# Scan stage of a hybrid SSD / Fourier layer: PSUM banks dealt out anew between the filling matrix products and the state products

## The chip, the cores and the metric

The kernel runs on one core of a Trainium2 chip. The metric is device time of one execution in microseconds (us). The kernel before takes 2252.82 us, the median of three runs (2246.53 to 2255.43). All readings below come from one further execution under the hardware profiler. Engines: PE is TensorE (matrix products), PEld its loading of weights, DVE is VectorE, ACT is ScalarE, POOL is GpSimd, SP is the engine from whose queue the DMAs are issued.

## The reference, cut to what matters

One layer over 1024 latent tokens and 256 context tokens of width 1024. The input projection feeds a bidirectional chunked state-space scan, a Fourier branch and two gates:

```python
u = h @ w_in[i]                                   # x, B, C | dt | z | Fourier | gates
states   = einsum('bcsgn,bcsgj,bcsgjp->bcgjpn', bc, decay_to_end, xdt)   # per chunk of 128
entering = scan(carry * dec + st)                                        # chunk after chunk
y_diag   = einsum('bcgjls,bcsgjp->bclgjp', cb[:, :, :, None] * lmat, xdt)
y_off    = einsum('bclgn,bcgjpn,bclgj->bclgjp', cc, entering, exp(a_cum))
y = (y_diag + y_off + d_skip * x) * silu(z)       # then grouped RMSNorm
mix = (gate0 * (y @ w_ssd_out) + gate1 * (f_mix @ w_fft_out)) @ w_o
```

There are 8 groups of 4 heads with 64 channels each, 8 chunks of 128 latent tokens and 2 of context, and two directions. After it come the residual, a SwiGLU feed-forward layer and the last norm.

## The kernel before, in words

The kernel is written against a tile framework: a program order is given, pools with a fixed number of buffers hold the tiles, and a scheduler that simulates time sets the order of the instructions on every engine and the waits between engines. A wait is kept by PSUM bank, not by address: two accesses of different engines to one bank are put one behind the other. [...]

The scan stage (the code from `phB = ExitStack()` on) does three kinds of PE work together:

- Filling products. `fill_stream` yields one piece after another of the input projection that the scan itself does not wait for at once: 12 weight blocks of `tm_units` (z and Fourier columns, 256 wide, eight token tiles each, so 96 tiles), and then five gate blocks of `gate_units` (j = 10 to 14, two PSUM tiles of 512 columns each). A tile of 256 columns is 24 products (8 blocks of k, three split products L203, L204, L205 in `mm3`). The z tiles (`fill` to `zs`) are read by ACT (tanh, L802) and then by DVE (L803), 64 of them. The Fourier tiles (`fill` to `ust`) are read by ACT alone (L807), 32 of them. All these use `fill_ps`, a pool of three banks.
- State products (`state_b`): for every group and step i, two products (L881, L882) of 128x256 go to the two halves of one bank `st`, of which there is one. DVE reads it in eight instructions (L891), which carry the running state `S` on.
- Outputs. Per tick n (group g, chunk c): `y_load` issues the DMA of `abc`, a broadcast of 512 KB from L900 that has two buffers. `y_a` makes `cb` (L908) and `yo` (L910, L911) on PE. ACT works over `abc` in eight instructions (L915), DVE in one (L917), ACT takes the exponential (L918), and DVE multiplies it with `cb` into `G` (L920). `y_b` multiplies `G` by x into `yd` (L943), `y_b2` finishes the row on DVE, ACT and POOL, and `y_c` transposes it (`ytr`, L968). `cb`, `yo`, `yd` and `ytr` have one bank each.

Together these are 3 + 1 + 4 = 8 banks. The loop over the ticks calls `state_a`, `state_b`, `y_a`, `y_b`, `y_c` and, last in each tick, `run_fill`, which draws pieces of the filling stream. What comes earlier in program order has priority in the scheduler.

Of the kernel before, what the change touches and what calls it, by code (L numbers as in the profile page):

```python
# [9 lines left out]
F32 = mybir.dt.float32  # L10
# [5 lines left out]
P = 128  # L16
# [125 lines left out]
def _build(nc, tc, h, o, hook, stop, es):  # L142
# [6 lines left out]
    def pool(name, side="left", bufs=1, space=None):  # L149
        kw = {} if space is None else dict(space=space)  # L150
        return tc.tile_pool(name=name, bufs=bufs, side=side, reuse_waits="tile", **kw)
# [38 lines left out]
    def wload(src, cols=1024):  # L190
        raw = wp.tile([P, 1024], F32, name="wraw", bufs=NRAW)
        nc.sync.dma_start(out=raw[:, :cols], in_=src)
        return wsplit(raw, cols)
# [8 lines left out]
    def mm3(ps, a, b, start, stop):  # L202
        nc.tensor.matmul(ps, lhsT=a[0], rhs=b[0], start=start, stop=False)  # L203
        nc.tensor.matmul(ps, lhsT=a[0], rhs=b[1], start=False, stop=False)  # L204
        nc.tensor.matmul(ps, lhsT=a[1], rhs=b[0], start=False, stop=stop)  # L205

    def mm3m(dsts, a, start, stop):
        for i, j in ((0, 0), (0, 1), (1, 0)):
            for ps, b in dsts:
                nc.tensor.matmul(ps, lhsT=a[i], rhs=b[j], start=start and (i, j) == (0, 0),  # L210
                                 stop=stop and (i, j) == (1, 0))
# [564 lines left out]
    ppg_ = hstack.enter_context(pool("ppg", "left", space=PSUM))  # L776
    pb = phB.enter_context(pool("pb", "right"))
    ppb = phB.enter_context(pool("ppb", "right", space=PSUM))
# [4 lines left out]
    ZSB, FOFF = 12, 4  # L783

    def fill_ps():
        return ppg_.tile([P, 512], F32, name="fill", bufs=3)

    zs_of = {}

    def tm_units(wi):  # L790

        w = [wload(h["wzf"][wi, kh]) for kh in range(2)]
        for t in range(NT):
            ps = fill_ps()[:, :256]
            for k in range(KT):
                hi, lo = w[k // 4]
                wsl = slice((k % 4) * 256, (k % 4) * 256 + 256)
                tsl = slice(t * P, t * P + P)
                mm3(ps, (h_hi[k][:, tsl], h_lo[k][:, tsl]), (hi[:, wsl], lo[:, wsl]), k == 0, k == KT - 1)
            if wi < NG:  # L800
                z = pb.tile([P, 256], F32, name="zs", bufs=ZSB)
                nc.scalar.activation(out=z, in_=ps, func=AF.Tanh, scale=0.5)  # L802
                nc.vector.scalar_tensor_tensor(out=z, in0=z, scalar=1.0, in1=ps, op0=ALU.add, op1=ALU.mult)  # L803
                zs_of[(wi, t)] = z
            else:
                u = pb.tile([P, 256], F32, name="ust", bufs=2)
                nc.scalar.copy(out=u, in_=ps)  # L807
                nc.sync.dma_start(out=s_u[wi - NG][:, t, :], in_=u)
            yield

    def gate_units(j):
        hi, lo = wload(h["wgate"][j])
        pss = [fill_ps() for _ in range(2)]
        for k in range(KT):
            sl = slice(k * P, k * P + P)
            mm3m([(pss[0], (h_hi[k][:, 0:512], h_lo[k][:, 0:512])), (pss[1], (h_hi[k][:, 512:], h_lo[k][:, 512:]))],
                 (hi[:, sl], lo[:, sl]), k == 0, k == KT - 1)
            if k == KT - 1:
                for hf in range(2):
                    gt = gtp.tile([P, 512], F32, name="gt", bufs=2)  # L820
                    nc.scalar.activation(out=gt, in_=pss[hf], func=AF.Tanh, scale=0.5)
                    nc.sync.dma_start(out=s_gate[j][:, 512 * hf:512 * hf + 512], in_=gt)
            if k % 2 == 1:
                yield
# [8 lines left out]
    class Group:  # L833
# [43 lines left out]
        def state_b(self, i):  # L877
            g, cf, cb = self.g, orf[i], orb[i]
            xf, xb = self.st.pop(i)
            st = ppb.tile([P, 512], F32, name="st", bufs=1)  # L880
            nc.tensor.matmul(st[:, 0:256], lhsT=self.Bt(cf), rhs=xf, start=True, stop=True)  # L881
            nc.tensor.matmul(st[:, 256:512], lhsT=self.Bt(cb), rhs=xb, start=True, stop=True)  # L882
            for d, S in ((0, self.Sf), (1, self.Sb)):
                sn = pb.tile([P, 256], F32, name=f"S{d}", bufs=9)
                sv_ = st[:, 256 * d:256 * d + 256]
                if i == 0:
                    nc.scalar.copy(out=sn, in_=sv_)
                else:
                    for j in range(HPG):
                        hd_ = slice(j * HD, j * HD + HD)  # L890
                        nc.vector.scalar_tensor_tensor(out=sn[:, hd_], in0=S[-1][:, hd_], scalar=decp[:, i, d, 4 * g + j:4 * g + j + 1],  # L891
                                                       in1=sv_[:, hd_], op0=ALU.mult, op1=ALU.add)
                S.append(sn)
# [85 lines left out]
    def fill_stream():  # L979
        yield from tm_units(0)  # L980
        jg = 2 * NGP
        for g in range(NG - 1):
            for _ in range(GSCHED[g]):
                yield from gate_units(jg)
                jg += 1
            if g in (1, 3, 5, 6):
                yield from tm_units(NG + (1, 3, 5, 6).index(g))
            yield from tm_units(g + 1)
        while jg < 15:
            yield from gate_units(jg)  # L990
            jg += 1

    fill = fill_stream()
# [228 lines left out]
    with pool("pd", "left") as pd_, pool("ppd", "left", space=PSUM) as ppd:  # L1222
# [29 lines left out]
        for kh in range(2):  # L1252
# [3 lines left out]
            for jd in range(8):  # L1256
                hi, lo = wload(h["wssd"][jd, kh])
                pss = [ppd.tile([P, 512], F32, name="dm", bufs=6) for _ in range(2)]
# [50 lines left out]
    with pool("pe", "left") as pe, pool("ppe", "left", space=PSUM) as ppe:  # L1309
# [3 lines left out]
        for dh in range(2):  # L1313
# [20 lines left out]
            for t in range(NT):  # L1334
                hf, tt = t // 4, t % 4
                ts_ = slice(tt * P, tt * P + P)
                ps = ppe.tile([P, 512], F32, name="em", bufs=3)
# [126 lines left out]
    for i in range(4):  # L1464
        t1, _, _, b22 = qd(i)
# [235 lines left out]
```

## Time and profile before

| | us |
|---|---|
| median of three runs | 2252.82 |
| the profiled execution | 2255.23 |
| its span on the core | 2253.5 |
| PE busy in the span | 2164.4 (96%) |
| PEld busy | 1809.4 (80%) |
| DVE busy | 1629.2 (72%) |
| ACT busy | 991.6 (44%) |
| POOL busy | 742.0 (33%) |

Times within the execution are counted from the start of the span. The scan stage lies between about 612 and 1165 us. An engine's row in a timeline gives the start, the length, the engine, the line, the operation and the tiles as out<-in; the bracket at its end is how long the engine sat idle before it, and what ended that.

### The profile page before, as it was taken

To read this page: it belongs to the slowest core of one execution; us is meant where nothing else is said; L and a number is where in the kernel's file an instruction comes from. 1 tells how busy PE (TensorE), PEld (TensorE's weight loads), DVE (VectorE), ACT (ScalarE), POOL (GpSimd) and SP (SyncE) were. 2 spreads that over 40 slices of the span, in tenths; PEclk is the share of its full clock that TensorE was granted. 3 is DMA by queue.
4 is the path that set the end of the run, shared out by engine and by line. 5 is a ranking of instruction groups with operands and counts; after the bars stand their busy time and mean duration, and the time that the engine had idled before them with its cause. 6 is when DMAs were issued, how large, how long until landed. Compare 5 with 4: busy or idle time off the path is not lost. (4 is left out here: it accounts for less than half of the span.)

```text
span 2253.5 us, 32731 instructions
## 1 busy us (share of the span) xinstructions
PE 2164.4 (96%) x11560; PEld 1809.4 (80%) x11560; DVE 1629.2 (72%) x2783; ACT 991.6 (44%) x2082; POOL 742.0 (33%) x610
## 2 busy tenths in 40 slices
PE   7999999999999999999999999998898999999997
PEld 1778888877889999999889887786676888887876
DVE  5888888997757777777636558826987567675578
ACT  4445444545345676676733212124422332334443
POOL 1532211010236455555521132144333333332222
PEclk8999999999999999999999999999899999999999
DMA  7222223333455455555454547541476234457765
GB/s 281 76 71 84 85 85 122 133 130 108 144 165 172 157 164 179 165 169 175 151 202 161 183 152 264 188 159 63 155 270 229 85 114 155 152 190 240 234 203 181
DMA packets 167101, 360.28 MB, mean 160 GB/s; under 512 B 17548, under 2 KB 57228, under 8 KB 166296
## 3 DMA queue, kind: packets, MB, share of 16 engines
q1 hardware_dynamic: 166936, 358.18, 47.7%
q8 instruction: 91, 1.49, 0.3%
q14 instruction: 74, 0.61, 0.1%
HBM read 267.34 MB, written 90.78 MB: 159 GB/s over the span
## 5 line engine op out<-in xcount | busy, mean ns | idle before, releaser
L199 POOL TENSOR_TENSOR wlo<-wraw,whi 128x1024 fp32r<-128x1024 f32 (+1 forms) x83 | 203.0, 2449 | 614.4 <-ACT whi L198 566.8
L203 PE MATMUL fill<-whi,hhi 128*128 128x256 f32 x768 | 222.4, 291 | 0.0
L198 ACT CAST whi<-wraw 128x1024 fp32r<-128x1024 f32 (+1 forms) x123 | 126.5, 1034 | 215.7 <-PE dm L210 82.9
L433 DVE SCALAR_TENSOR_TENSOR cv<-pad,vecs,cv 128x1282 f32<-128x1282 f32 (+1 forms) x128 | 211.0, 1678 | 9.1 <-ACT cv L430 8.7
L204 PE MATMUL fill<-wlo,hhi 128*128 128x256 f32 x768 | 215.8, 281 | 0.6 <-POOL wlo L199 0.6
L205 PE MATMUL fill<-whi,hlo 128*128 128x256 f32 x768 | 216.0, 282 | 0.0
L915 ACT ACTIVATE abc<-abc,a_all 128x128 f32<-128x128 f32 x512 | 157.8, 390 | 96.2 <-DMA abc<-s_a 93.4
L203 PE MATMUL fp<-m,oph 128*128 128x512 f32 x452 | 180.3, 400 | 12.5 <-ACT oph L1384 10.5
L205 PE MATMUL fp<-m,opl 128*128 128x512 f32 x452 | 180.4, 400 | 9.6 <-DVE opl L1385 6.7
L204 PE MATMUL fp<-m,oph 128*128 128x512 f32 x452 | 180.2, 399 | 0.0
L496 PE MATMUL mm<-tq,whi 128*128 128x512 f32 x480 | 153.9, 401 | 2.3 <-ACT whi L198 2.3
L203 PEld LDWEIGHTS fill<-whi,hhi 128*128 128x128 f32 x768 | 144.1, 188 | 2.2 <-ACT ust L807 0.4
L204 PEld LDWEIGHTS fill<-wlo,hhi 128*128 128x128 f32 x768 | 144.6, 188 | 1.6 <-POOL wlo L199 0.8
L205 PEld LDWEIGHTS fill<-whi,hlo 128*128 128x128 f32 x768 | 144.3, 188 | 0.5
L496 PE MATMUL mm<-hhi,whi 128*128 128x512 f32 x320 | 128.2, 402 | 3.4 <-DVE pad L572 3.4
L496 PE MATMUL mm<-hlo,whi 128*128 128x512 f32 x320 | 127.6, 399 | 0.0
L496 PE MATMUL mm<-hhi,wlo 128*128 128x512 f32 x320 | 127.6, 400 | 0.0
L203 PEld LDWEIGHTS fp<-m,oph 128*128 128x128 f32 x452 | 85.9, 190 | 34.2 <-ACT oph L1384 11.7
L205 PEld LDWEIGHTS fp<-m,opl 128*128 128x128 f32 x452 | 85.6, 189 | 33.8 <-DVE opl L1385 9.7
L917 DVE COPY_PREDICATED abc<-misc,abc 128x512 f32<-128x512 int32 x64 | 50.8, 793 | 85.0 <-ACT abc L915 84.8
L496 PEld LDWEIGHTS mm<-tq,whi 128*128 128x128 f32 x480 | 89.7, 189 | 23.7 <-ACT whi L198 3.4
L891 DVE SCALAR_TENSOR_TENSOR S<-S,ead,st 128x64 f32<-128x64 f32 x512 | 104.7, 271 | 0.0
(411 smaller groups left out, 5929.4 us busy)
## 6 DMA issues: line engine op xcount, KB each, us to landing
abc<-s_a SPq DMA_DIRECT2D x64, 512.0 KB
fraw<-in_wfi SPq DMA_DIRECT2D x44, 512.0 KB
wraw<-in_wxbc SPq DMA_DIRECT2D x32, 512.0 KB
dx<-in_wada SPq DMA_DIRECT2D x32, 512.0 KB
wraw<-in_wzf SPq DMA_DIRECT2D x24, 512.0 KB
gt<-s_gate SPq DMA_DIRECT2D x24, 512.0 KB
fi<-in_wfo SPq DMA_DIRECT2D x22, 512.0 KB
s_cw<-fo SPq DMA_DIRECT2D x44, 256.0 KB
```

Source lines behind the costliest of these rows:

```text
L198: nc.scalar.copy(out=hi[:, :cols], in_=raw[:, :cols])
L199: (eng or nc.gpsimd).tensor_tensor(out=lo[:, :cols], in0=raw[:, :cols], in1=hi[:, :cols].bitcast(F32), op=ALU.subtract)
L203: nc.tensor.matmul(ps, lhsT=a[0], rhs=b[0], start=start, stop=False)
L204: nc.tensor.matmul(ps, lhsT=a[0], rhs=b[1], start=False, stop=False)
L205: nc.tensor.matmul(ps, lhsT=a[1], rhs=b[0], start=False, stop=stop)
L433: nc.vector.scalar_tensor_tensor(out=v[:, :n], in0=pd[:, t:t + n], scalar=cwh[:, 5 * b + t:5 * b + t + 1], in1=v[:, :n], op0=ALU.mult, op1 ...
L496: nc.tensor.matmul(ps, lhsT=lhs[x], rhs=b[i][y], start=i == 0 and (x, y) == (0, 0), stop=i == 3 and (x, y) == (1, 0))
L891: nc.vector.scalar_tensor_tensor(out=sn[:, hd_], in0=S[-1][:, hd_], scalar=decp[:, i, d, 4 * g + j:4 * g + j + 1], in1=sv_[:, hd_], op0=AL ...
L915: nc.scalar.activation(out=abc[:, d, j, :], in_=abc[:, d, j, :], func=AF.Identity, scale=-1.0, bias=a_all[:, c, hd:hd + 1])
L917: nc.vector.copy_predicated(out=E, mask=tri_b.bitcast(mybir.dt.int32)[:, None, :].to_broadcast([P, HPG, P]), data=abc[:, 1])
```

## The change

Three edits, all in the scan stage. The filling pool shrinks from three banks to two, and two successive tiles of 256 columns of one weight block (t even, t odd) are now the two halves of one bank. The state products get a second bank. Gate blocks with odd j (11 and 13) take both banks of the state pool in place of the filling pool's. The count of banks stays eight (2 + 2 + 4), and no instruction is added or taken out; the scheduler makes a new order of them.

```diff
     def fill_ps():
-        return ppg_.tile([P, 512], F32, name="fill", bufs=3)
+        return ppg_.tile([P, 512], F32, name="fill", bufs=2)
+
+    def st_ps():
+        return ppb.tile([P, 512], F32, name="st", bufs=2)
...
         for t in range(NT):
-            ps = fill_ps()[:, :256]
+            if t % 2 == 0:
+                bank = fill_ps()
+            ps = bank[:, 256 * (t % 2):256 * (t % 2) + 256]
...
-        pss = [fill_ps() for _ in range(2)]
+        pss = [(st_ps if j % 2 else fill_ps)() for _ in range(2)]
...
-            st = ppb.tile([P, 512], F32, name="st", bufs=1)
+            st = st_ps()
```

Line numbers of the changed kernel are 3 higher than before from `tm_units` on and 5 higher from there to the end. Three places of the new order follow. The names are tiles with their numbers; `whi`, `wlo` are the split weights, `hhi`, `hlo` the split inputs.

PE at the start of the scan, before. Each `fill` number is one tile of 256 columns in a bank of its own:

```order
L203 MATMUL fill_4981<-whi_4971,hhi0_190 128x256 [waits DVE_49,Activation_49]
...
L203 MATMUL fill_5026<-whi_4971,hhi0_190 128x256 [waits DVE_49]
...
L203 MATMUL fill_5071<-whi_4971,hhi0_190 128x256
...
L203 MATMUL fill_5116<-whi_4971,hhi0_190 128x256 [waits DVE_49]
...
L908 MATMUL cb_5350<-cT_5322,bT_5320 128x128 [waits DMAHW5_49,DMAHW4_49]
L910 MATMUL yo_5352<-S0_4959,cT_5322 128x256
```

The first `cb` stands behind eight whole tiles. The same place now, where a `fill` number is a bank with two tiles:

```order
L203 MATMUL fill_5070<-whi_4971,hhi0_190 128x256 [waits DVE_49]
...
L203 MATMUL fill_4981<-whi_4971,hhi0_190 128x256 [waits DVE_49]
...
L913 MATMUL cb_5346<-cT_5318,bT_5316 128x128 [waits DMAHW5_49,DMAHW4_49,PE_49]
L203 MATMUL fill_5159<-whi_4971,hhi0_190 128x256 [waits DVE_49]
...
L887 MATMUL st_5102<-xwb_5054,bh_4935 128x256 [waits DMAHW6_49,Pool_49]
L948 MATMUL yd_5536<-xh_4921,G_5361 128x64 [waits DVE_49]
L948 MATMUL yd_5536<-xh_4921,G_5361 128x64 x3
L913 MATMUL cb_5546<-cT_5318,bT_5316 128x128 [waits DVE_49]
```

The first `cb` now stands behind three tiles, and the first `yd` behind five tiles, five pairs of state products, that `cb` and one of the two `yo` products.

PE in the fifth group, before: the third tile (`fill_8374`) ends, the products of a tick follow, and the fourth tile (`fill_8468`) starts without a wait:

```order
L205 MATMUL fill_8374<-whi_8247,hlo7_205 128x256
L943 MATMUL yd_8402<-xh_7248,G_8304 128x64 [waits DVE_49,PE_49]
...
L908 MATMUL cb_8416<-cT_8318,bT_8316 128x128 [waits DMAHW4_49,DMAHW2_49]
L910 MATMUL yo_8418<-S0_7623,cT_8318 128x256 [waits DVE_49]
L911 MATMUL yo_8418<-S1_7980,cT_8318 128x256
L881 MATMUL st_8449<-xwf_8322,bh_8161 128x256 [waits DMAHW1_49,DVE_49,PE_49]
L882 MATMUL st_8449<-xwb_8323,bh_8165 128x256 [waits DMAHW3_49,Pool_49]
...
L203 MATMUL fill_8468<-whi_8241,hhi0_190 128x256
```

The same group now: the fifth tile (first half of bank `fill_8537`) has ended, and the sixth (its second half) starts after the products of a tick and 15 products of the seventh (`fill_8658`):

```order
L205 MATMUL fill_8537<-whi_8223,hlo7_205 128x256
L973 MATMUL ytr_8746<-misc_171,yz_8382 128x128 [waits Activation_49]
...
L948 MATMUL yd_8820<-xh_7242,G_8711 128x64 [waits DVE_49]
L948 MATMUL yd_8820<-xh_7242,G_8711 128x64 x3
L913 MATMUL cb_8834<-cT_8725,bT_8723 128x128 [waits DMAHW3_49,DMAHW0_49,DVE_49]
L915 MATMUL yo_8836<-S0_8046,cT_8725 128x256 [waits DVE_49]
L203 MATMUL fill_8658<-whi_8217,hhi0_190 128x256 [waits DVE_49]
...
L203 MATMUL fill_8537<-whi_8217,hhi0_190 128x256 [waits DVE_49]
L204 MATMUL fill_8537<-wlo_8218,hhi0_190 128x256
```

The second half's first product waits for DVE, that is for the reading of the first half, and the products of the next bank were moved ahead of it.

ACT at the same place of the changed kernel: the reading of the fourth tile (`fill_8349`, second half) and of the fifth (`fill_8537`, first half):

```order
L920 ACTIVATE abc_8861<-abc_8861,a_all_210 128x128 [waits DMAHW4_49]
L920 ACTIVATE abc_8861<-abc_8861,a_all_210 128x128 x7
L807 ACTIVATE zs_8467<-fill_8349 128x256 [waits PE_49]
L923 ACTIVATE abc_8861<-abc_8861 128x512 [waits DVE_49]
L807 ACTIVATE zs_8562<-fill_8537 128x256 [waits PE_49]
L976 ACTIVATE yst_8652<-ytr_8746,vecs_173 128x128 [waits PE_49]
```

Between the readings of the two tiles there is one exponential and no further group of eight `abc` instructions.

## Rows read from the trace of the kernel before

**Rows 1.** Windows by stage: stretch, its length, busy time (and count) of each engine.

```profile
612.00:692.00 80.00, 74.49 (x543) 69.80 (x542) 51.54 (x162) 34.41 (x90) 32.51 (x34) 0.98 0.52 166
692.00:1090.00 398.00, 388.15 (x2946) 370.71 (x2946) 298.98 (x957) 269.41 (x838) 213.88 (x257) 1.00 0.52 166
1090.00:1165.00 75.00, 74.50 (x377) 61.87 (x376) 30.48 (x81) 42.02 (x122) 29.56 (x33) 1.00 0.51 166
1165.00:2253.50 1088.50, 1041.71 (x4859) 845.16 (x4857) 744.38 (x1049) 365.59 (x668) 332.09 (x220) 0.99 0.53 180
```

**Rows 2.** Waits of PE from 612 to 692: total us, times, longest.

```profile
PE cb L908 <- DVE cd L924: 1.5, 1, 1.5
PE yo L911 <- DVE S L891: 1.4, 1, 1.4
PE st L881 <- DVE S L891: 1.2, 1, 1.2
```

**Rows 3.** Waits of PE from 692 to 1090.

```profile
PE st L881 <- DVE S L891: 6.3, 9, 1.4
PE st L881 <- PE ytr L968: 1.8, 2, 0.9
PE yo L911 <- DVE S L891: 1.6, 1, 1.6
```

**Rows 4.** Waits of PE from 1165 to the end, of 15 rows the second.

```profile
PE fp L205 <- DVE opl L1385: 6.7, 6, 2.7
```

**Rows 5.** Timeline of PE at the start and in the fifth group: start us, us.

```profile
612.22 0.28 PE L203 MATMUL fill<-whi,hhi 128*128 128x256 f32 x1
...
617.83 0.28 PE L203 MATMUL fill<-whi,hhi 128*128 128x256 f32 x1
...
873.89 1.00 PE L943 MATMUL yd<-xh,G 128*128 128x64 f32 x8
874.72 0.44 PE L908 MATMUL cb<-cT,bT 128*128 128x128 f32 x2
875.00 0.60 PE L910 MATMUL yo<-S,cT 128*128 128x256 f32 x2
875.43 0.59 PE L911 MATMUL yo<-S,cT 128*128 128x256 f32 x2
875.86 0.59 PE L881 MATMUL st<-xwf,bh 128*128 128x256 f32 x2
...
885.61 0.28 PE L205 MATMUL fill<-whi,hlo 128*128 128x256 f32 x1
```

**Rows 6.** Timeline of ACT at the start of the scan.

```profile
619.70 0.66 ACT L802 ACTIVATE zs<-fill 128x256 f32<-128x256 f32 x2 [3.35 <-DMA s_gate<-pad]
...
632.13 2.45 ACT L915 ACTIVATE abc<-abc,a_all 128x128 f32<-128x128 f32 x8 [4.18 <-DMA abc<-s_a]
...
634.87 1.28 ACT L918 ACT_TABLE_LOAD   x1
636.16 0.63 ACT L918 ACTIVATE abc<-abc 128x512 f32<-128x512 f32 x1
```

**Rows 7.** Timeline of ACT in the fifth group, fifth tile.

```profile
886.23 0.63 ACT L918 ACTIVATE abc<-abc 128x512 f32<-128x512 f32 x1
886.75 1.04 ACT L198 CAST whi<-wraw 128x1024 fp32r<-128x1024 f32 x1
887.69 2.46 ACT L915 ACTIVATE abc<-abc,a_all 128x128 f32<-128x128 f32 x8
890.04 0.37 ACT L802 ACTIVATE zs<-fill 128x256 f32<-128x256 f32 x1
```

**Rows 8.** Timeline of DVE in the fifth group, fifth tile.

```profile
891.24 0.40 DVE L803 SCALAR_TENSOR_TENSOR zs<-zs,fill 128x256 f32<-128x256 f32 x1
891.57 0.67 DVE L920 TENSOR_TENSOR G<-abc,cb 128x512 f32<-128x512 f32 x1
```

**Rows 9.** Waits of ACT from 692 to 1090, the first.

```profile
ACT abc L915 <- DMA abc<-s_a: 72.2, 38, 4.1
```

## The prediction

> **What bounds the kernel now.** The windows by stage come first, because the change touches one stage only. The scan stage is the first three windows, 612 to 1165 us [rows 1]. Length less PE's busy time is PE's idle time: 80 − 74.49 = 5.51 us, 398 − 388.15 = 9.85 us, 75 − 74.50 = 0.50 us, together 15.9 us of 553. PE bounds the stage, and no order of the instructions can give back more than these 15.9 us: that is 0.7% of the whole. ACT is busy for 269.41 and DVE for 298.98 of the middle window's 398 us, so both have room on average; what matters is how late they are at one place. The granted clock is 0.98, 1.00 and 1.00 of full speed, so there is nothing to gain by the clock.
>
> The waits of PE come next, to see what the 15.9 us are. The products of L881 wait for DVE, which still reads the one state bank: 1.2 us at the start [rows 2] and 6.3 us in nine waits later [rows 3]. Two more of L881's waits, 1.8 us, are for the transpose L968 ahead of it on PE [rows 3]. L911 waits for S 1.4 and 1.6 us, L908 for `cd` 1.5 us [rows 2, 3]. No row is a filling product that waits for a bank: three filling banks are enough today.
>
> The timelines come last, for prices. From 612.22 to 617.83 us PE runs 48 filling products, two tiles: 5.61/48 = 0.117 us each, 2.8 us a tile [rows 5]. The four `yd` products of a tick take 874.72 − 873.89 = 0.83 us, `cb` 0.28 us, a `yo` product 0.43 us and the pair 0.86 us [rows 5]; the state products have the shape of `yo`, and I price them alike.
>
> **The change, part by part.**
>
> *State products, second bank.* The pair of step i+1 no longer waits for DVE to finish with step i. That removes what stands as "st L881 <- DVE S": 1.2 + 6.3 = 7.5 us [rows 2, 3]. What is late next is the chain of S itself: DVE's eight instructions of a step follow one another, and L911 needs S. With a deeper pool the state products run earlier, which helps `yo` as well, but DVE's work is not shortened. Best case: 7.5 and the 1.8 behind the transpose, and the `yo` and `cb` waits of 1.4 + 1.6 + 1.5 us, −13.8 us; worst case the waits only move, 0. I take −7, the direct row less a remainder.
>
> *Start of the scan.* In the new order the first `yd` stands behind five tiles, five pairs of state products, one `cb` and one `yo`. PE's own work up to there is 120 × 0.117 = 14.0, 5 × 0.86 = 4.3, 0.28 and 0.43: 19.1 us, so PE is there at 612.2 + 19.1 = 631.3 us. `yd` needs G(0), which needs the broadcast `abc` to have landed: ACT sat idle 4.18 us for that DMA, and began at 632.13 [rows 6]. The DMA is not moved forward by the change. From 632.13: 2.45 us for the eight instructions, a table load and the exponential until 636.16 + 0.63 = 636.8 [rows 6], and 0.67 us for G on DVE [rows 8]: about 637.5. So PE must lose about 6 us before its first `yd`, where before it had eight whole tiles ahead of `cb` and three banks in hand. The wait on the first shared bank is part of these 6 us, not on top: ACT reads the first z tile at 619.70 only, since it waits for a DMA to `s_gate` [rows 6]; with 0.37 on ACT and 0.40 on DVE [rows 7, 8] the first half is read at about 620.5, 2.7 us after the 617.83 at which PE has two tiles done [rows 5]. Another 0.7 us I allow for the bank behind the second group of `abc`. Against it stands what the early order serves sooner: of the waits of 1.5 and 1.4 us [rows 2] most goes, −2.5. Net 6 + 0.7 − 2.5 = +4.2; I take +4. Ends: 0 if PE's order is slack enough that the later waits are all saved, and +7 if nothing comes back.
>
> *New waits at the shared banks.* 96 tiles make 48 pairs. The second half's first product now waits until ACT, and for z tiles DVE too, have read the first half. The trace of before has no such wait, so its price comes from one place in the fifth group. There the tile's last product starts at 885.61 [rows 5], and its reading by DVE ends at 891.24 + 0.40 = 891.64 [rows 8]: 6.0 us. Of these ACT spent 2.46 on a group of eight `abc` instructions and 1.04 on a cast that stood in front of the reading [rows 7]. In the new order one exponential stands between, no group of eight; that gives 6.0 − 2.46 − 1.04 = 2.5 us. What covers it on PE at that place is the tick's four `yd`, `cb`, one `yo` and 15 products of the next bank: 0.83 + 0.28 + 0.43 + 15 × 0.117 = 3.3 us (the transpose left out). So the slack is 0.8 us: the wait is nothing if ACT keeps the order's time, and 6.0 − 3.3 = 2.7 us if ACT is as late as it is today. Why ACT would be late is in its waits: 38 times it waited for the broadcast `abc` to land, 72.2 us, 1.9 on average and up to 4.1 [rows 9], and every reading queued behind that waits too. The order was made with DMAs on time. I estimate how often: 48 pairs with 2.5 us each of exposed time are 120 us out of the 478 us from 612 to 1090, a quarter; a quarter of 38 waits is about 10 that meet a pair, and each overruns the slack by 1.9 − 0.8 = 1.1 us at most, 0.8 as a mean since a wait rarely falls wholly inside. 10 × 0.8 = +8 us. Ends: 0 (all covered), and 48 × 2.7 = +130 us (each pair as at that place before), of which the row nearest to the new order, 2.5 against 3.3, is close to the low end; hence +8.
>
> [...]
>
> *Gate blocks 11 and 13* use the state banks: each has two tiles of 512 columns and so takes both; the state products of a tick then queue behind a gate block's reading. The last window has 0.50 us of PE idle [rows 1], and the filling pool has two banks for the even blocks meanwhile. I take 0; ends −0.5 (all that is idle there) and +3 (two blocks by 1.4 us, the longest wait for a state bank [rows 3]).
>
> *Behind 1165 us* the work is the same, in a slightly other order. The products L205 there wait 2.7 us at the longest for DVE [rows 4]: 0 ± 3.
>
> Sum: −7 + 4 + 8 + 0 + 0 = +5 us. The profiled execution took 2255.2 us, so 2260; the median of the runs, 2252.8, lies 2.4 below it, and the same sum there gives 2258. A measurement here can tell about 0.5%, 11 us, from no change, so this is "the same".
>
> **The rivals.**
>
> *A, slower: the bank wait comes again and again.* One mechanism: `abc` lands late, ACT waits for it in order, the reading of a first half stands behind, and PE, whose order has the second half next, has no third bank to turn to. It decides once ACT lags by more than the slack of 0.8 us at most pairs. For it: 38 waits of a mean 1.9 us, more than twice that slack [rows 9]. Against it: the new order puts ticks and the next bank's products in between, and today's idle PE has no bank wait at all. Price: 48 × 0.9 (half of 1.9) = 43 us, in place of the 8: 2253 − 7 + 4 + 43 = 2293; with waits that meet half of the pairs 2272.
>
> *B, faster: the idle time goes.* PE finds the state bank free, `yo` and `cb` follow sooner, and the start hides behind tiles as it does now. For it: all rows of waits in the middle window hang on the state chain [rows 3]. Against it: the start's DMA [rows 6], and that a third filling bank was what kept PE fed. Price: the −13.8 above with nothing against it, 2239.
>
> *C: the change does not do what it says.* The state wait moves to L911, which waits for the same serial work of DVE on S, and the two new terms stay: 0 + 4 + 8 = +12, 2265. For it: L911's waits for S of 1.4 and 1.6 us are as long as L881's longest, 1.4 [rows 2, 3], so the two wait for one chain. Against it: most of the nine waits in the middle window are short ones, 6.3/9 = 0.7 us, which a step's lead covers.
>
> **How the numbers follow.** The forecast case has 0.52, A 0.15, B 0.17, C 0.16. The likeliest is 2258, with its own range 2247 to 2268: −6 if the banks never make PE wait and the start costs 2 less, and 10 more if the bank waits are twice as many. The range for 8 in 10 reaches to most of B (2241) and to the part of A in which half of the pairs or a little more wait (2284). Below 2241.6 counts as faster: most of B, 0.15 in all. Above 2264.1 counts as slower: all of A, a little over half of C and 0.08 of the forecast case's upper end, 0.32. The rest, 0.53, is the same.
>
> **What the profile after would show.** First step right: the row of state products that wait for DVE's S is gone or under 1 us, and L911's wait for S is no longer than 3 us; under C that one has grown to 6 or more. Start: the first `yd` near 637 us, and PE idle in the window 612 to 692 about 9.5 us instead of 5.5. Banks: new rows of filling products (L203) that wait for DVE's reading of `zs` or ACT's of `ust`, 8 us in about ten waits; under A 20 to 45 us in over twenty, with ACT's idle time before them ended by the `abc` DMA; under B none. PE's busy time in the stage should not change. The forecast is wrong if PE idles in 692 to 1090 by less than 5 or more than 20 us, or if the stage behind 1165 us moves by more than 3 us: then the new order did something there that I priced at nothing.

## The result: slower by 0.9%

The changed kernel takes 2273.83 us (median of four runs, 2271.19 to 2278.02). The ratio to the kernel before is 1.0092, 95% interval 1.0065 to 1.0119. The profiled execution took 2273.01 us, its span 2271.2; before it was 2255.23 and 2253.5, so the spans differ by 17.7 us. The sign of the forecast was right, the size was not: 2258 had been forecast as the likeliest. The time lies outside the forecast's own range (2247 to 2268), in the part that the prediction called slower (above 2264.1, chance 0.32), and inside the range for 8 in 10 (2241 to 2284). That it is close to the half-way case of rival A (2272) is a coincidence, as the terms below show.

### The profile page after: what moved, and what is told of

Its sections match the earlier page's. It is cut to its first block, busy times and chain, and to the rows that moved or that the text cites. A ratio compares the mean times of both kernels' runs of the same rounds, so it can differ in the third digit from the quotient of the medians.

```text
span 2271.2 us, 32775 instructions
## 1 busy us (share of the span) xinstructions
PE 2172.2 (96%) x11560; PEld 1815.6 (80%) x11560; DVE 1618.1 (71%) x2783; ACT 995.1 (44%) x2082; POOL 743.0 (33%) x610
## 5 line engine op out<-in xcount | busy, mean ns | idle before, releaser
L920 ACT ACTIVATE abc<-abc,a_all 128x128 f32<-128x128 f32 x512 | 158.6, 390 | 117.2 <-DMA abc<-s_a 110.7
L203 PE MATMUL fp<-m,oph 128*128 128x512 f32 x452 | 180.3, 400 | 10.4 <-DVE hold L1442 10.4
L203 PEld LDWEIGHTS fp<-m,oph 128*128 128x128 f32 x452 | 85.9, 190 | 31.4 <-ACT oph L1389 10.8
```

The costliest lines, as they stand in the source:

```text
L920: nc.scalar.activation(out=abc[:, d, j, :], in_=abc[:, d, j, :], func=AF.Identity, scale=-1.0, bias=a_all[:, c, hd:hd + 1])
```

## The profile after, and where the time went

The windows by stage, with the stage's ends moved to the same work (columns as in [rows 1]):

```profile
612.00:692.00 80.00, 74.10 (x530) 69.34 (x529) 55.13 (x198) 37.00 (x102) 32.61 (x39) 0.98 0.49 160
692.00:1110.00 418.00, 394.09 (x2914) 371.86 (x2913) 296.51 (x940) 273.03 (x839) 216.42 (x255) 0.98 0.51 161
1110.00:1185.00 75.00, 73.52 (x394) 62.35 (x394) 24.77 (x59) 36.90 (x106) 26.73 (x29) 1.00 0.44 144
1185.00:2271.00 1086.00, 1045.66 (x4882) 850.18 (x4881) 738.94 (x1050) 367.58 (x670) 332.31 (x220) 0.99 0.54 181
```

The start is as before [rows 1]: 5.90 us of idle PE against 5.51. The middle window is 20 us longer and has 23.91 us idle where there were 9.85, and its granted clock is 0.98 where it was 1.00. To cut the stage by the work and not by round numbers, I take it from the first filling product to the first product behind it (`sab`, L1103 before, L1108 after). The next two fences are one window each, from 611 us to that product, before and after:

```profile
611.00:1164.51 553.51, 537.66 (x3862) 502.66 (x3861) 381.54 (x1199) 345.40 (x1048) 276.45 (x324) 1.00 0.52 166
```

```profile
611.00:1190.63 579.63, 547.84 (x3861) 508.19 (x3859) 377.39 (x1197) 348.00 (x1048) 275.75 (x323) 0.98 0.50 160
```

The scan stage went from 552.3 to 579.0 us, +26.7. PE's idle time went from 15.9 to 31.8 us, +15.9; PE's busy time rose by 10.2 us for the same products, of which the clock explains 7.9 (below); the other 2.3 us stay unexplained. Behind `sab` the rest became shorter: 1089.0 us before, 1080.6 after, -8.4. With a start 0.6 us earlier this makes the 17.7.

PE's waits of the changed scan from 611 us to `sab` (total, times, longest), where [rows 2] and [rows 3] have those of before:

```profile
PE fill L203 <- DVE zs L808: 9.2, 11, 2.3
PE fill L203 <- ACT whi L198: 4.8, 4, 1.9
PE ytr L973 <- ACT yst L976: 4.7, 4, 1.5
PE fill L203 <- ACT ust L812: 3.8, 2, 2.6
PE cb L913 <- DMA cT<-s_cT: 2.8, 1, 2.8
PE yo L915 <- DVE y L934: 2.7, 3, 1.3
PE yd L948 <- DVE G L925: 1.1, 3, 0.4
PE yd L948 <- DVE yz L956: 0.9, 1, 0.9
PE fill L204 <- POOL wlo L199: 0.8, 1, 0.8
```

The state products' wait for DVE's S is gone, as forecast. In its place stand rows that the kernel before did not have: filling products that wait for a tile's reading (`zs`, `ust`), and, which I had not priced, filling products that wait for the cast of the next weights (`whi`) and transposes that wait for `yst`. Casts, `ust` and `yst` are ACT's work, and DVE's step on `zs` follows ACT's on the same tile; the `yo` and `yd` rows are DVE's own.

One place shows the mechanism. The timeline of ACT, then of PE, around 731 us (start, length, what was done; idle before and its releaser in the bracket):

```profile
731.00 2.44 ACT L920 ACTIVATE abc<-abc,a_all 128x128 f32<-128x128 f32 x8 [4.84 <-DMA abc<-s_a]
733.35 0.89 ACT L966 ACTIVATE yz<-yz,grs 128x256 f32<-128x256 f32 x2
734.15 0.35 ACT L812 COPY ust<-fill 128x256 f32<-128x256 f32 x1
```

```profile
731.32 0.59 PE L916 MATMUL yo<-S,cT 128*128 128x256 f32 x2
734.55 0.58 PE L203 MATMUL fill<-whi,hhi 128*128 128x256 f32 x1 [2.64 <-ACT ust L812]
...
735.15 0.41 PE L205 MATMUL fill<-whi,hlo 128*128 128x256 f32 x1
735.36 0.41 PE L203 MATMUL fill<-whi,hhi 128*128 128x256 f32 x1
735.58 0.41 PE L204 MATMUL fill<-wlo,hhi 128*128 128x256 f32 x1
```

ACT had nothing to do for 4.84 us, because the broadcast `abc` had not landed. Behind its eight instructions stood `yz` and then a copy of 0.35 us. By the program's order, in which the tiles have their numbers, this copy reads the second half of the bank `fill_6053`, and the product at 734.55 is the first one of the first half of `fill_6405`, which takes over that bank. PE waited 2.64 us for the copy. So this is not a second half that waits for its first half: it is a new tile that waits for a bank to come free.

The whole scan looks like that. Laid beside the program's order, 3 of the 13 waits for `zs` and `ust` stand at the start of a second half (4.5 us, of which 2.3 are the first wait of the scan) and 10 at the first half of a new bank (8.5 us). The order explains it. Because a second half waits for the reading of its first half, the scheduler put a tile of the other bank between them, and so the first half of a new bank follows right behind the second half that had the same bank. Between the last product of a tile and the first product of the next tile in that bank PE has 24 filling products (the median; one tile's worth) if the next is a second half, but 9 if it is the first half of a new bank. The kernel before had 48 in the median, two tiles' worth. The order printed above the prediction has one such place: `fill_8658` starts with a wait for DVE, ahead of the second half of `fill_8537`.

The other thing is in the starts of the products after it: 735.15, 735.36, 735.58, 0.213 us apart in the mean of ten steps (735.15 to 737.28), where the same products stand 0.117 us apart in [rows 5]. Two windows of this place, idle and then slow (third number: PE's busy time; third from the end: the granted clock):

```profile
732.00:735.00 3.00, 0.45 (x2) 0.45 (x3) 1.52 (x3) 3.00 (x10) 0.30 (x1) 0.85 0.00 0
735.00:737.50 2.50, 2.50 (x14) 2.50 (x14) 1.39 (x6) 1.20 (x6) 0.96 (x2) 0.50 0.34 109
```

PE idles for 2.55 of 3 us, and then it runs at a granted clock of 0.50 of full speed until about 737.5. The steps between the starts go with it: 0.213 us at 0.50 and 0.117 us at 1.00 (the clock of the kernel before from 612 to 618 us), 1.8 times as long. Counted in windows of 2 us from 612 to 1092, with what each one's clock lacks to 1.00 put down as time at 0.50, the changed kernel has 20.4 us at 0.50, in which by this count 9.3 us of work are lost (what the clock lacks times PE's busy time); the kernel before had 3.4 us and 1.4. That is +7.9 us, a price that my sum did not have. The changed kernel's own four runs go the same way: granted clock 0.988, 0.986, 0.985, 0.983 with 2271.2, 2273.0, 2274.7, 2278.0 us.

The theories that the experiments were made for, before the waits were sorted by halves: T1: the second half's wait costs the time. T2: two banks in place of three cost it. T3: the new order does, the state products above all. Later T4: ACT's lateness behind the `abc` DMA does, which shared banks expose.

## The experiments

The table has the measured ratio to the kernel before with its interval, and from each profile the scan stage (first filling product to `sab`), PE's idle time in the window from 611 us to `sab`, PE's direct waits for the readers of filling tiles (`zs`, `ust`), the time at a clock of 0.50 from 612 to 1092 us (counted as above), and the stretch from the first `fp` product of the feed-forward part to the last.

| kernel | median us | ratio | scan | idle | readers | clock 0.50 | fp |
|---|---|---|---|---|---|---|---|
| before | 2252.8 | | 552.3 | 15.9 | 0 | 3.4 | 673.7 |
| the change | 2273.8 | 1.0092 [1.0065, 1.0119] | 579.0 | 31.8 | 13.0 | 20.4 | 664.5 |
| 1 three shared banks, one state bank | 2258.6 | 1.0039 [1.0023, 1.0054] | 566.7 | 25.8 | 10.4 | 6.8 | 663.8 |
| 2 not shared | 2259.2 | 1.0039 [1.0024, 1.0054] | 558.4 | 19.0 | 11.5 | 3.4 | 674.1 |
| 3 one state bank | 2276.6 | 1.0106 [1.0084, 1.0127] | 568.2 | 26.4 | 7.3 | 6.8 | 670.9 |
| 4 readings paired | 2255.1 | 1.0022 [1.0010, 1.0035] | 559.3 | 19.6 | 2.9 | 3.4 | 674.3 |
| 5 third `abc` | 2279.5 | 1.0129 [1.0102, 1.0156] | 575.1 | 31.4 | 9.6 | 6.8 | 673.3 |
| 6 before, third `abc` | 2255.5 | 1.0016 [1.0002, 1.0029] | 556.6 | 18.2 | 2.2 | 6.8 | 672.9 |
| 7 before, `st` and `ytr` share two | 2256.5 | 1.0020 [1.0002, 1.0038] | 551.2 | 15.4 | 0 | 6.8 | 671.7 |
| 8 gates on filling banks | 2274.9 | 1.0101 [1.0085, 1.0116] | 575.7 | 27.5 | 10.5 | 23.8 | 665.8 |
| 9 the change, one `abc` load | 2248.2 | 0.9980 [0.9964, 0.9996] | 548.0 | 13.3 | 1.7 | 6.8 | 674.6 |
| 10 before, one `abc` load | 2243.5 | 0.9956 [0.9941, 0.9971] | 541.5 | 9.4 | 1.7 | 0 | 673.8 |
| 11 whole-bank readings | 2250.6 | 0.9992 [0.9976, 1.0009] | 550.1 | 14.9 | 1.0 | 0 | 673.5 |
| 12 the same, three and one | 2244.6 | 0.9958 [0.9940, 0.9976] | 552.8 | 14.3 | 0 | 10.2 | 665.7 |

A profile is one execution; where it lay far from its kernel's median (3: 9 us below, 5: 4 below, 4: 7 above, 6 and 7: 6 above, 9: 5 above, 12: 4 above), the median counts. The ratios go by the runs of the kernel before on the same chip. The edits of 1 to 5, 8, 9, 11 and 12 are made in the changed kernel, those of 6, 7 and 10 in the kernel before.

**1. Three shared banks, one state bank.**

```diff
+        return ppg_.tile([P, 512], F32, name="fill", bufs=3)
...
+        return ppb.tile([P, 512], F32, name="st", bufs=1)
...
+        pss = [fill_ps() for _ in range(2)]
```

> Three filling banks with two tiles each, one state bank, all gate blocks on the filling banks: of the change only the sharing is left. Measured so far: from the first filling product of the scan to the first product behind it (L1103, in the changed kernel L1108) 552.3 us before and 579.0 us with the change. Theory T1 (the halves: a second half waits until the first half is read, whatever the number of banks): filling products still wait for DVE's zs and ACT's ust, 8 us or more together, and the scan takes 562 us or more. Rival T2 (the count: two banks in place of three): with three banks these waits are 3 us or less and the scan is within 5 us of 552, with the state products' waits of 7.5 us back.

The filling products wait for readers 10.4 us (5.9 and 4.5) although there are as many banks as before, and the scan is 14 us longer than before. T2 as the whole cause falls. A third bank ends neither kind of wait: of the 14 waits 5 stand at second halves (4.2 us) and 9 at the first half of a new bank (6.2 us).

**2. The sharing undone.**

```diff
-            if t % 2 == 0:
-                bank = fill_ps()
-            ps = bank[:, 256 * (t % 2):256 * (t % 2) + 256]
+            ps = fill_ps()[:, :256]
```

> Two filling banks with one tile of 256 columns each, two state banks, gate blocks as in the change: only the sharing is undone. T1 (the halves cost): the second halves' wait is gone, filling products wait for their readers less than in the change (13.0 us there), scan under 570 us. T2 (the count): two buffers of any size give the same cover, one tile of 2.8 us; waits of filling products for DVE and ACT 13 us or more, scan 575 to 595 us, no better than the change.

The scan is 558.4 us, 21 less than with the change, so two banks with one tile each are better than two with two. But T1 was half wrong: the direct waits hardly fell, 13.0 to 11.5 us. Here every tile takes over a bank, with one tile's worth of filling products (24, the median) in between, and all 15 waits stand there. What went are other waits. PE's waits from 611 us to `sab`:

```profile
PE fill L203 <- DVE zs L806: 7.7, 10, 2.2
PE fill L203 <- ACT ust L810: 3.8, 5, 1.3
PE st L884 <- issue: 2.3, 1, 2.3
PE yo L913 <- DVE y L932: 1.5, 2, 0.8
```

No row of `whi` (4.8 us with the change), and half a microsecond of transposes (4.7); and 3.4 us at a clock of 0.50 for 20.4. That these hang on the order that sharing forces is argued, not shown: the scheduler made another order for every kernel here.

**3. One state bank.**

```diff
+        return ppb.tile([P, 512], F32, name="st", bufs=1)
...
+        pss = [fill_ps() for _ in range(2)]
```

> The change without the second state bank (seven banks in all; gate blocks then use the filling banks): T1 and T2 alike say that the filling waits stay at about 13 us and that the state products wait for DVE's S again, 6 to 10 us, so the scan is 583 to 590 us, 4 to 10 longer than with the change. Rival T3 (the scheduler's order, not the fill banks: with a second state bank the state products run ahead and push filling products, cb and yo out of place): without the second state bank the scan falls back to 552 to 565 us.

No theory is met. The state products wait for S again (7.0 us), the readers cost 7.3. The profiled run took 2267.5 us at a clock of 0.988, the other three 2276.3 to 2277.2 at 0.984 to 0.986; by the median the kernel is 2.8 us slower than the change, within the spread. But its feed-forward part is 6.4 us longer (last column), so what the second state bank is worth in the scan is not settled. T3 is not borne out by the median.

**4. Readings paired**: both halves are read behind the products of the second.

```diff
+            rd.append((t, ps))
+            if t % 2:
+                for tt, pr in rd:
...
+                        nc.scalar.activation(out=z, in_=pr, func=AF.Tanh, scale=0.5)
...
+                rd = []
             yield
```

> The change, but the readings of both halves stand behind the products of the second half in program order, so that a second half never waits for a reader; the same instructions. T1: waits of filling products for DVE and ACT under 4 us, half clock in the scan under 6 us, scan 545 to 560 us, whole time 2235 to 2260. T2: the bank is then free only after four readings, with 5.6 us of cover by the other bank; waits 8 us or more, scan over 565 us. T3: the order is what costs, scan about 575 us, with PE waiting for ytr, whi and cT as in the change.

T1's numbers, all three: readers 2.9 us, 3.4 us at a clock of 0.50, scan 559.3. The same banks and the same instructions are 18.7 us faster by the medians than the change (0.7%, 16 us, by the ratios). PE's waits for `fill` on ACT in this scan; there is no row for `zs`:

```profile
PE fill L203 <- ACT whi L198: 2.9, 3, 1.5
PE fill L203 <- ACT ust L816: 2.9, 2, 1.4
```

In its order the two halves of a bank stand one behind the other, and between the first half of a new bank and the tile that had the bank stand 48 filling products (the median), as in the kernel before. So it is for the most part not sharing as such that costs (7 us of the scan's 26.7 are left). It is the reading of each half by itself, with the order that the scheduler makes from it; the direct wait of second halves was the smaller part (4.5 of 13.0 us in the change).

**5 and 6. A third buffer for abc, in the change and in the kernel before.**

```diff
-            abc = pb.tile([P, 2, HPG, P], F32, name="abc", bufs=2)
+            abc = pb.tile([P, 2, HPG, P], F32, name="abc", bufs=3)
```

> The change with a third buffer for abc, so that its DMA can be issued a tick earlier; nothing else. Theory T4 (ACT takes its work in order and waits for the abc DMA, 110.7 us in the scan with the change; casts of weights, readings of filling tiles and the copies of yst stand behind, and with the shared banks PE has nothing else to do): ACT's wait for the DMA falls below 50 us, PE's idle time in the scan from 31.8 to 20 us or less, half clock mostly gone, scan 579 to 560 or less, whole time 2250 to 2260. T1 in its narrow form (the wait for the reading of a first half itself, whatever ACT waits for): idle time 27 us or more, scan 573 or more, whole time 2267 or more.

> The kernel before with a third buffer for abc. T4: three filling banks already hide most of ACT's lateness, so the gain is small: 0 to 8 us of 2250 (the waits for DVE's S, 7.5 us, are not ACT's). If it gains as much as the change does (15 us or more), the late DMA is a cost of its own and no part of the explanation of the change.

The first does not test T4, since the wait that was to fall did not: ACT still waits 106.1 us for the DMA (110.7 in the change), for the DMA stands in SP's queue behind others, and SP still waits for `cd` ahead of it (78.5 us). The narrow T1's numbers were all met (idle time 31.4, scan 575.1, whole time 2279.5 us), which for the same reason decides nothing. The kernel before gains nothing either.

**7. The kernel before, `st` and `ytr` in two banks in turn.**

```diff
-            st = ppb.tile([P, 512], F32, name="st", bufs=1)
+            st = ppb.tile([P, 512], F32, name="st", bufs=2)
...
-            tp = ppb.tile([P, 512], F32, name="ytr", bufs=1)
+            tp = ppb.tile([P, 512], F32, name="st", bufs=2)
```

> The kernel before, with two banks that the state products and the transposes share in turn (in place of one for each): the filling pool keeps its three banks of one tile. The second state bank by itself: if the waits of 7.5 us for DVE's S were worth their row (the prediction's first term), scan 552 to 545 or less and whole time 4 to 8 us less. If DVE's serial work on S is what is waited for (rival C), the waits stay or move to yo and the time is within 3 us of before; transposes that wait for state banks could make it up to 5 us longer.

PE's waits in the scan:

```profile
PE st L968 <- DVE S L891: 11.4, 9, 3.1
PE fill L203 <- ACT whi L198: 1.3, 2, 0.8
```

The state products hardly wait any more, but the transposes (L968), which now use the same banks, wait 11.4 us for the same readings by DVE. The scan is 551.2 us, 1 less. The wait moved; this is rival C's way, though by the transposes and not by `yo`, so it does not settle what an unmixed second bank is worth.

**8. Gate blocks back on the filling banks.**

```diff
-        pss = [(st_ps if j % 2 else fill_ps)() for _ in range(2)]
+        pss = [fill_ps() for _ in range(2)]
```

> The change with the gate blocks 11 and 13 on the filling banks, as before. The gate term was priced at 0 (-0.5 to +3). All theories on the sharing: within 5 us of the change (2273.8). If it is more than 5 us faster, the gate blocks on the state banks cost that; if slower, they saved it (waits of gate products for ACT's gt were 2.9 us in the run with one state bank).

1.1 us from the change by the medians (ratios 1.0101 and 1.0092): the gate term of 0 holds as well as these runs can tell.

**9 and 10. abc loaded once, in the change and in the kernel before.**

```diff
+            if not abc0:
+                t = pb.tile([P, 2, HPG, P], F32, name="abc0", bufs=1)
+                nc.sync.dma_start(out=t.rearrange("p a b c -> p (a b c)"),
...
+                abc0.append(t)
+            self.abc = pb.tile([P, 2, HPG, P], F32, name="abc", bufs=2)
...
+                    nc.scalar.activation(out=abc[:, d, j, :], in_=abc0[0][:, d, j, :], func=AF.Identity, scale=-1.0, bias=a_all[:, 0, 32 * d + j:32 * d + j + 1])
```

> The change, with the broadcast abc loaded for the first tick alone; later ticks compute on that tile (their decay terms are those of the first tick; ACT, DVE and PE do as much as before, 63 DMAs of 512 KB are left out). So ACT never waits for that DMA, which the third buffer had not achieved (its wait was 106.1 us with it). To be read against the same edit in the kernel before. Theory T4 (the shared banks cost time because ACT is late): PE's idle time in the scan falls from 31.8 to 18 us or less, no more than one stretch at half clock, and the change's kernel is within 8 us of its partner. T1, narrow (the second half waits for the first half's reading even when ACT is on time): filling products still wait 10 us or more, and the change's kernel stays 15 us or more behind its partner.

> The kernel before with the same part left out (abc loaded for the first tick alone). PE was idle for 15.9 us in the scan and 10.6 of these were waits for DVE's S, which remain in part; the start, where the first abc is still loaded, is as it was. T4 and T1: 2240 to 2252, a gain of at most 10 us.

With the change 2248.2 us, without 2243.5: of the 20 us between the two kernels 4.7 are left when ACT hardly waits for that DMA any more (once, 4.7 and 3.4 us). The kernel before gains 10 us by it, the change 26. In the scan 6.5 us (548.0 and 541.5) are left of 26.7. The window from 611 us to `sab` of the change's kernel, and then its waits:

```profile
611.00:1161.17 550.17, 536.90 (x3866) 504.34 (x3865) 401.19 (x1198) 349.78 (x1048) 286.44 (x324) 0.99 0.34 107
```

```profile
PE st L888 <- DVE xwf L880: 4.2, 1, 4.2
PE yo L919 <- DVE y L938: 3.0, 2, 2.7
PE fill L203 <- DVE zs L808: 1.7, 2, 1.0
```

The banks are shared as in the change, and the readers cost 1.7 us in place of 13.0; no `whi`, no `ytr`. T4's numbers for the idle time (18 us or less) and for the distance of the two kernels (within 8 us) are met, the narrow T1's are not. There are two stretches at a clock of 0.50, one more than T4 allowed. One reservation: 63 DMAs of 512 KB are gone, and the traffic fell from 160 to 107 GB/s, which may bring the weights sooner too (not measured). That the wait itself, and not the traffic, did all of it is not separated.

**11 and 12. One reading for a whole bank, with the change's banks and with those of before.**

```diff
+            if t % 2:
+                if wi < NG:
+                    z = pb.tile([P, 512], F32, name="zs", bufs=ZSB // 2)
+                    nc.scalar.activation(out=z, in_=bank, func=AF.Tanh, scale=0.5)
...
+                    zs_of[(wi, t - 1)], zs_of[(wi, t)] = z[:, :256], z[:, 256:]
```

and for 12 also `fill` with three banks, `st` with one, and the gate blocks on `fill`.

> The paired readings once more, but with one reading of 512 columns in place of two of 256 for each bank (ACT 48 and DVE 32 instructions fewer; zs and ust tiles are pairs). Banks as in the change (2 filling, 2 state). If ACT's and DVE's lateness is what is left: 2245 to 2253, 2 to 10 us less than the paired kernel's 2255.1. If the later reading of the first halves delays the rows of y (ACT's zs of a tick comes a tile later): 2255 to 2265.

> The same with the banks dealt as before: three filling banks, now with two tiles each, and one state bank; gate blocks on the filling banks. With 11 us of cover for each reading no filling product should wait (under 1 us), the waits for DVE's S (7.5 us) stay: scan 545 to 552, whole time 2240 to 2250, the fastest of all. If the second state bank is worth more than the third filling bank, it is slower than the kernel with two and two.

11 came as expected if lateness is what is left: 2250.6 us, which is the time of the kernel before. 12 is the fastest kernel that computes the whole layer, 0.9958 of before, and the version to keep. But not for the reason expected: its scan took 552.8 us, no less than before (its profile lay 4 us above its median, that of before 2). The waits of 12 in the scan:

```profile
PE st L888 <- DVE S L898: 6.8, 7, 1.9
PE fill L203 <- ACT whi L198: 2.9, 3, 1.4
PE ytr L975 <- ACT yst L978: 1.6, 2, 1.0
```

No wait for a reader, as expected, and the wait for S as before. Its lead of 6.0 us on 11 is less than what the last column of the table gives it.

**The last column.** The feed-forward part was not touched, and yet its stretch falls into two heaps: 663.8 to 665.8 us in four kernels (the change, 1, 8, 12; mean 665.0) and 670.9 to 674.6 in ten (mean 673.3). Sorted by the order in which SP issues the DMAs `fraw`, `fi` and `s_cw` there, the fourteen fall into the same two heaps: the scheduler made one of two sequences for that place. The waits that [rows 4] stands for shrink with it; in the changed kernel, from 1185 us on:

```profile
PE fp L205 <- DVE opl L1390: 1.2, 2, 1.0
```

1.2 us for 6.7. By this sorting about 8 us of the change's time were given back by an order far behind the edit (8.3 between the heaps, 9.2 in its own profile), and 12's lead on 11 is of the same size. No kernel changed that order alone; it is a sorting of fourteen profiles without an exception, not an experiment.

## Why the prediction was right in sign and too small

The sum forecast +5 us, all of it idle time of PE in the scan. By the profiled spans the idle time rose by 15.9 us, PE's busy time, which "should not change", by 10.2, and behind the scan 8.4 came back: 15.9 + 10.2 - 8.4 = 17.7. Two of the signs that the prediction named for being wrong are there: PE idles for 20.8 us from 692 to 1090 (20 was the limit), and the stage behind the scan moved by 8.4 us (3 was the limit). That the time still lies in the range for 8 in 10 is partly luck, for without the 8.4 us the spans would differ by 26.

- **State products, -7.** The rows went, 7.6 + 1.8 = 9.4 us. But in the same scan transposes wait 4.7 us for `yst` and `yd` 2.0 us where there was nothing, and the `yo` and `cb` waits, 5.3 us before, are 2.7 for `y` and 2.8 for the DMA of `cT`. These four changes sum to -2.5, so this term was too good by 4.5. "What is late next" I had named as S; it was ACT, a DMA and DVE's work on the rows.
- **Start, +4.** The first `yd` was forecast at 637 us:

```profile
619.67 0.38 PE L203 MATMUL fill<-whi,hhi 128*128 128x256 f32 x1 [2.30 <-DVE zs L808]
627.23 0.46 PE L913 MATMUL cb<-cT,bT 128*128 128x128 f32 x2 [2.76 <-DMA cT<-s_cT]
637.76 1.00 PE L948 MATMUL yd<-xh,G 128*128 128x64 f32 x8
```

It came at 637.76, and the wait on the first shared bank was 2.30 us (2.7 forecast). But the time came out right by another path than the forecast one: `yd` itself did not wait, PE's loss stood at the first shared bank and ahead of `cb`, for the DMA of `cT`, and until 692 the idle time rose by 0.4 us only, in place of the 4 forecast: the credit was larger than the 2.5 taken.

- **Waits at the shared banks, +8.** This step failed: its place was wrong, and what stands beside the readings was left out. The readers cost 13.0 us in 13 waits; without the first one, which the start's term has, 10.7 in 12, close to the 8 in ten. That is luck. The term priced the second halves, with a tick's products and 15 of the next bank as cover, and outside the start only 2 of the 12 waits stand there (2.2 us); 10 stand at the first half of a new bank (8.5 us), where the order has the least cover and the sum had no price at all. Beside them PE waits 5.6 us for casts (`whi` 4.8, `wlo` 0.8; before 0.6): ACT's queue has the next weights' cast in it too, as the row I used for the price already showed [rows 7]. ACT itself was later, too: its waits for `abc` grew from before to after (windows from 611 us to `sab`):

```profile
ACT abc L915 <- DMA abc<-s_a: 93.4, 46, 9.4
```

```profile
ACT abc L920 <- DMA abc<-s_a: 110.7, 53, 6.4
```

- **The clock, not in the sum.** "Nothing to gain by the clock" was true and beside the point: there was something to lose, 7.9 us by the windows. It is the largest loss that the sum had at nothing.
- **Gate blocks, 0.** Right by experiment 8.
- **Behind 1165 us, 0 ± 3.** Wrong: -8.4 us, by the DMA order in the feed-forward part. The scheduler's order differs there too, and I took "the same work" for the same time.
- **The rivals.** A's chain is what happened, from a late `abc` over ACT's queue to PE (the place at 731 us, experiment 9), but not where A has it, since most waits are for a bank to come free, and not as often: A was to show 20 to 45 us in over twenty waits, and 13.0 us in 13 came. B fell. C fell as it was stated: no `yo` product waits for S any more (3.0 us before), so the state wait did not move there; but other waits took its place.

As shown: the reading of each half by itself, with its order (4), and ACT's lateness behind `abc`, with the reservation on the traffic (9 against 10), cost most of it. As argued only: that the order's short cover at a new bank is what lets the lateness through, and that each stretch at a clock of 0.50 came from the idle time just ahead of it.

## What to carry to other kernels

Two tiles in one PSUM bank, each read as soon as it was done, were not two more buffers here: PE waited 13.0 us in 13 waits for their readers, 4.5 us at second halves and 8.5 us at first halves of new banks. Look in the new order at every tile that takes over a bank, the first half of the next pair too, and count the work that stands between it and the reading it waits for; where that was short here (9 products in the median), PE waited most (10 of the 13 waits). If a bank is to be shared, read it behind its last product: that took most of the loss back here (18.7 us by the medians). Price a new wait by everything that stands in the reader's queue, add what a lower clock may cost after idle time (7.9 us by the windows here), and compare the new order of the stages that the edit doesn't touch (8.4 us here).

## What the runs showed that I had not expected

- Idle PE may cost more than itself: after 2.55 of 3 us idle at 732 us the clock was 0.50 of full speed for 2.5 us. But the total of the idle time does not decide: experiment 5 had 31.4 us idle and 6.8 us at 0.50, experiment 8 had 27.5 and 23.8.
- Runs of one kernel differ, and the clock granted to them with them: experiment 3 took 2267.5 us at 0.988 and 2277 at 0.984.
- One reading of 512 columns for a bank cost ACT less than two of 256: ACT was busy 342.0 us in the scan of 11 against 348.6 in 4, for 48 instructions fewer.
